# A decoder trunk on one core: down products in two halves of 256 columns, their stationary tiles shifted by 128 bytes, and one wide step per block

## The chip, the core and the metric

The kernel runs on one core of a Trainium2 chip. TensorE (PE in the profile) multiplies, VectorE (DVE) and ScalarE (ACT) work on what it makes, GpSimd (POOL) and SyncE (SP) mostly issue transfers. The metric is the device time of one execution in microseconds, the median of several. Before the change it is 1897.52 us (three runs, 1895.87 to 1897.72).

## The reference

Two layers over 512 tokens of 1024 features in float32. Each layer is: half-step SwiGLU feed-forward, token mixer (differential attention in layer 0, pooling in layer 1), cross-attention into 256 memory tokens, and a second half-step SwiGLU; after each, a layer norm of `a * x + ...`. So there are four feed-forward blocks, and the change touches these alone:

```python
def swiglu_ffn(x, w_in, w_out):
    h = x @ w_in                       # 1024 -> 2 x 2816
    g, u = jnp.split(h, 2, axis=-1)
    return (jax.nn.silu(g) * u) @ w_out   # 2816 -> 1024
```

## The kernel before

**Products in three passes.** Every float32 operand is split into a high part (a cast on ACT) and a low part (a subtraction on DVE). A product is then three matmuls, high by high, high by low, low by high, all into the same PSUM bank:

```python
def mm3(self, out, w, x, start, stop, again=False):        # L227
    self.first_mm = mm(out, w[0], x[0], ...)                # L231
    mm(out, w[0], x[1], ...)                                # L232
    self.last_mm = mm(out, w[1], x[0], ...)                 # L233
```

`w` is the stationary operand (a slice of 128 columns, 512 bytes per partition, which PE loads ahead of the matmul) and `x` the moving one. In the profile's rows an instruction stands as `out<-moving,stationary`.

**A feed-forward block.** The hidden width is cut into 11 units of 256. Products are not done plainly: seven products of sub-blocks take the place of eight, on the up side (`up`, seven products x, y, z of 24 matmuls each with 256 moving columns) and on the down side (`down`, for two units at a time, seven steps px, py, pz). In an up product the weights wh, wl are stationary and the factors of x (xh, xl, or the tiles xe) move. In a down step it is the reverse: h (tiles ha and hb) is stationary and the weights move, 512 columns at a time. A down step is two products (b = 0, 1) of two contraction chunks (k = 0, 1) of three passes, so 12 matmuls; DVE adds each product's bank to the tokens X (L935).

**The order of work.** `FFN_TURNS` gives five turns: three units up; then four turns with two units up and, beside them, the down steps of two earlier units. Units 8, 9 and 10 go down at the end of the block in plain products (`plain_down`, ps). The generators of a turn are stepped one after the other (the loop of `ffn` from L629), which puts on PE: 24 matmuls of one unit, 24 of the other, one down step, and again. A turn has seven such rounds; in the last turn the last two down steps stand among plain products. So a block has 4 turns x 7 = 28 down steps, the kernel 112, with 1344 matmuls. A scheduler behind the program then places every instruction on its engine's queue; `queue_behind(a, b)` makes `a` stand behind `b` on one engine.

**Places in memory.** Tiles lie one behind the other. `APART["ffn"]` is 64, `ROUND` 512: a pad of 64 bytes ahead of the weights (`to_w`), and one of 448 ahead of x's factors (`_x`, `to_x`). With them the weights start at 32 modulo 512 bytes, all factors of x at 480, and the tiles behind xe (hb, sp, ha, sr, hr) at 480 too. All tiles and slices used here are multiples of 512 bytes long, so a tile's start tells where each of its slices lies modulo 512.

Of the kernel before, what the change touches and what calls it, by code (L numbers as in the profile page):

```python
# [17 lines left out]
P = 128  # L18
D = 1024
S = 512  # L20
# [26 lines left out]
    turn=(1.0, 1.0, 1.2, 1.5),  # L47
# [79 lines left out]
class Trunk:  # L127
# [49 lines left out]
    @contextmanager  # L177
    def phase_pool(self, gain, spare, **bufs):

        self.gain, self.spare, self.bufs, self.phase = gain, spare, bufs, {}
        with ExitStack() as ctx:
            for t in bufs:
                if t == "_x":
                    self.to_x(ctx)
                elif t == "_w":
                    self.to_w(ctx)
                else:
                    self.phase[t] = self.stage.get(t) or ctx.enter_context(self.pool(t))  # L190
            yield
# [378 lines left out]
    def ffn(self, layer, j, ln, beside=()):  # L570
        w_in, w_out = self.a["ffn_w_in"][layer, j], self.a["ffn_w_out"][layer, j]
        self.seven_of, self.factors = {}, self.factor_tiles()
        nc, n, beside = self.nc, len(FFN_TURNS), iter(beside)
        at_start = bool(self.load_rest)
        downs = {i: self.down(d, w_out, 2.0 * ALPHA if i == 1 else 1.0) for i, (_, d) in enumerate(FFN_TURNS) if d}

        def start(turn):
            ups = FFN_TURNS[turn][0]

            early = (2, 1, 1) if turn == 0 else (0, 0)  # L580
            rest = self.load_rest.pop if turn == 0 and at_start else lambda: lambda: None
            got = [self.up(w_in, u, lane, early[lane], rest() if lane == 0 else None) for lane, u in enumerate(ups)]
            for lane, g in enumerate(got):
                next(g)
                if lane == 1:
                    rest()()
            if turn > 1:
                next(downs[turn])
            return got + [downs[i] for i in downs if i == turn]

        works = start(0)
        if at_start:

            zeros = self.act("hb", (P, P + S), mybir.dt.bfloat16)
            nc.vector.memset(zeros, 0.0)
            idle = self.aux("idle", "yz")
            self.warm(zeros, idle, 7)
            for tag, half in (("px", 0), ("py", 1)):
                for t in self.late[:2]:
                    self.turn(t, half, tag)  # L600
                if half == 0:
                    with self.tc.issue_after(self.last_turn.ins):
                        self.warm(zeros, idle, 9)
                next(works[0])
                if half == 0:
                    next(works[0])
            next(works[1])
        else:
            for w in works + works[:1]:
                next(w)  # L610
            self.turn_late(2)
        self.late = []
        next(works[0])
        act, dve = self.first_split
        if self.begins:

            for late, first in zip(self.begins, (act, dve)):
                self.queue_behind(late, first)
        second = self.second_factors()
        if at_start:  # L620

            next(works[0])
            for w in (works[1], second, second, works[1], works[2], works[2], works[0]):
                with self.behind():
                    next(w)
        else:
            for w in (second, *works[1:], second, downs[1]):
                next(w)
        for turn in range(n):  # L629
            behind = turn == n - 1  # L630
            for step in range(1 if turn == 0 else 0, 9 if behind else 7):
                if turn == 0 and (step == 3 or step == 2 and at_start):
                    next(second)
                if step == 4:
                    if behind:
                        coming = [self.plain_down(w_out, layer, j, ln, beside)]
                    else:
                        coming = start(turn + 1)
                        if at_start and turn == 0:
                            with self.tc.issue_after(self.last_load.ins):  # L640
                                next(downs[1])
                if behind and step in (4, 6, 7, 8):
                    next(coming[0])
                if behind and step > 3:
                    few(beside, 2)

                for lane, w in enumerate(works[: None if not behind or step > 1 else -1]):
                    if not (at_start and turn == 0 and lane < 2 and step == 1):
                        next(w, None)
                    if turn == 0 and lane == 1 and step == 2 and at_start:  # L650
                        next(works[0])
                    if turn == 0 and lane == 0 and step == 2 and not at_start:
                        next(second)
                    if at_start and turn == 0 and lane == 0 and step == 3:
                        next(works[2])
                if turn == 1 and step == 3:
                    self.seven_of[self.waiting[0]] = self.seven(self.waiting[1])
            works = coming
        drain(works[0])
# [63 lines left out]
    def up(self, w, u, lane, early, between):  # L723
# [28 lines left out]
        def product(ps, v, a, start=False, passes=False):  # L752
            if passes or between and start and a == 0:
                by_passes(ps, v, a)
                return
            x = self.factors[a]
            for j in range(2):
                o = slice(j * P, (j + 1) * P)
                for k in range(4):

                    self.mm3(
                        ps[:, j], (v[0][:, k, o], v[1][:, k, o]), (x[0][:, k], x[1][:, k]),
                        start and j == k == 0, j == 1 and k == 3, True,
                    )

        def by_passes(ps, v, a, which=range(3)):

# [14 lines left out]
        at_start = early > 0 and self.begins is None  # L782
        sp = lambda: self.tmp("ha" if third else "sp", (P, 2, H))
# [38 lines left out]
        hr = self.tmp("hr", (P, 2, S))  # L822
# [73 lines left out]
    def down(self, pairs, w, scale):  # L896
# [24 lines left out]
        def product(ps, b, a, ws, start=False):  # L921

            o = slice(b * P, (b + 1) * P)
            for k in range(2):
                h, l = hs[k][a]
                self.mm3(ps, (h[:, o], l[:, o]), ws[k], start and k == 0, k == 1, not start)

        started = set()

# [802 lines left out]
        return self.stage_pools(5, dict(raw=raw), order)  # L1732

    def ffn_phase(self, **more):
        bufs = dict(b1=1, b3=1, b2=1, b4=1, _x=0, xe=6, hb=4, sp=4, ha=4, sr=1, hr=3)
        return self.phase_pool(("hr", "sr"), "sp", **bufs, **more)

    def ffn_first(self, layer, ln):
# [84 lines left out]
```

## Time and profile before

| | before |
|---|---|
| median of the runs | 1897.52 us |
| the profiled execution | 1899.25 us |
| its span, first to last instruction | 1897.5 us |
| granted TensorE clock | 0.999 |
| PE busy | 1886.5 us in 13120 matmuls |
| DVE busy | 1540.9 us (81%) |
| ACT busy | 1000.8 us (53%) |
| POOL busy | 308.2 us (16%) |
| HBM | 147 GB/s over the span |

PE's busy time is the union of its matmuls' modelled spans, which overlap: a busy PE need not be at its best pace. What a matmul costs in a full stream is the distance between the starts of neighbours, read from the rows in order of time.

### The profile page before, as it was taken

The page shows a single profiled execution, that of the slowest core. Times are in us where ns is not written, and L with a number is a line of the kernel's source. Part 1 is how long each engine was busy: PE and PEld are TensorE (multiplying, and loading weights), DVE is VectorE, ACT ScalarE, POOL GpSimd, SP SyncE. Part 2 cuts the span into 40 slices and gives each one's busy share as a digit, 9 for nine tenths or more (in the row PEclk, how much of TensorE's full clock was granted, in tenths as well). Part 3 has the DMA queues.
Part 4 walks back from the last instruction along what each step waited for, and adds up shares of the span by engine and source line. Part 5 has one row for each costly group of instructions (what it writes and reads, how often), then busy time and mean ns, then how long its engine had stood idle before and what let it go on. Part 6 is the DMA issues. An engine that isn't in the chain of part 4 may idle for free.

```text
span 1897.5 us, 32589 instructions
## 1 busy us (share of the span) xinstructions
PE 1886.5 (99%) x13120; PEld 1730.9 (91%) x13120; DVE 1540.9 (81%) x2246; ACT 1000.8 (53%) x1542; POOL 308.2 (16%) x274
## 2 busy tenths in 40 slices
PE   9999999999999999999999999999999999999998
PEld 8999998888889988999998999999899889999996
DVE  7888989888876558889887988898786568998886
ACT  6555554566654435555554655555455436555552
POOL 3112120112110002221220311212120012211210
PEclk9999999999999999999999999999999999999999
DMA  9978772322235327987785687777464438867861
GB/s 254 215 178 178 171 141 85 103 69 75 91 112 178 112 70 181 195 177 168 144 188 168 118 179 181 168 166 162 157 172 146 142 69 180 173 159 178 185 129 53
DMA packets 250055, 283.20 MB, mean 149 GB/s; under 512 B 8752, under 2 KB 213040, under 8 KB 249904
## 3 DMA queue, kind: packets, MB, share of 16 engines
q0 software_dynamic: 94080, 94.38, 32.3%
q1 hardware_dynamic: 155824, 186.74, 30.2%
q8 instruction: 103, 1.69, 0.4%
q14 instruction: 48, 0.39, 0.1%
HBM read 274.79 MB, written 4.19 MB: 147 GB/s over the span
## 4 chain that ended last, share of the span: by engine, by line
PE 96%; DMA 2%; DVE 1%; ACT 0%; SPq 0%; issue 0%; POOL 0%; DVEq 0%; ACTq 0%
PE x L231 7%; PE x L232 7%; PE x L233 7%; PE ps L231 5%; PE ps L233 4%; PE ps L232 4%; PE z L231 4%; PE z L233 4%; PE z L232 4%; PE px L233 3%; PE px L231 3%; PE px L232 3%; PE x L773 3%; PE y L231 2%; PE y L232 2%; PE y L233 2%
## 5 line engine op out<-in xcount | busy, mean ns | idle before, releaser
L741 POOL DMA_DIRECT2D ra<-in_ffn_w_in_dram x132 | 170.7, 1307 | 977.6 <-DVE wl L748 960.4
L746 ACT CAST wh<-ra 128x1024 fp32r<-128x1024 f32 x176 | 184.9, 1053 | 197.8 <-PE x L232 63.8
L748 DVE TENSOR_TENSOR wl<-ra,wh 128x1024 fp32r<-128x1024 f32 x176 | 214.2, 1220 | 64.7 <-ACT wh L746 64.0
L231 PE MATMUL x<-xe,wh 128*128 128x256 f32 x704 | 195.0, 277 | 0.0
L232 PE MATMUL x<-xe,wh 128*128 128x256 f32 x704 | 194.8, 277 | 0.0
L233 PE MATMUL x<-xe,wl 128*128 128x256 f32 x704 | 194.8, 277 | 0.0
L746 ACT CAST wh<-rc 128x1024 fp32r<-128x1024 f32 x132 | 138.9, 1053 | 100.3 <-PE x L232 41.6
L143 ACT CAST wh<-b 128x1024 fp32r<-128x1024 f32 x112 | 117.8, 1052 | 134.8 <-PE x L232 62.2
L748 DVE TENSOR_TENSOR wl<-rc,wh 128x1024 fp32r<-128x1024 f32 x132 | 159.5, 1218 | 24.7 <-ACT wh L746 24.7
L144 DVE TENSOR_TENSOR wl<-b,wh 128x1024 fp32r<-128x1024 f32 x112 | 136.7, 1220 | 40.9 <-ACT wh L143 40.9
L231 PE MATMUL x<-xh,wh 128*128 128x256 f32 x536 | 148.7, 277 | 0.0
L232 PE MATMUL x<-xl,wh 128*128 128x256 f32 x536 | 148.4, 277 | 0.0
L233 PE MATMUL x<-xh,wl 128*128 128x256 f32 x536 | 148.4, 277 | 0.0
L231 PEld LDWEIGHTS x<-xe,wh 128*128 128x128 f32 x704 | 132.4, 188 | 1.3
L232 PEld LDWEIGHTS x<-xe,wh 128*128 128x128 f32 x704 | 132.3, 188 | 1.3
L233 PEld LDWEIGHTS x<-xe,wl 128*128 128x128 f32 x704 | 132.2, 188 | 0.0
L144 DVE TENSOR_TENSOR wl<-raw,wh 128x1024 fp32r<-128x1024 f32 x64 | 78.5, 1233 | 45.8 <-ACT wh L143 45.2
L231 PEld LDWEIGHTS x<-xh,wh 128*128 128x128 f32 x536 | 100.8, 188 | 0.7
L232 PEld LDWEIGHTS x<-xl,wh 128*128 128x128 f32 x536 | 100.8, 188 | 0.7
L233 PEld LDWEIGHTS x<-xh,wl 128*128 128x128 f32 x536 | 100.7, 188 | 0.0
L143 ACT CAST wh<-raw 128x1024 fp32r<-128x1024 f32 x64 | 66.4, 1049 | 62.5 <-PE xq L232 18.2
L231 PE MATMUL z<-xe,wh 128*128 128x256 f32 x352 | 97.5, 277 | 0.0
(445 smaller groups left out, 6239.9 us busy)
## 6 DMA issues: line engine op xcount, KB each, us to landing
ra<-in_ffn_w_in_dram POOLq DMA_DIRECT2D x132, 512.0 KB, 7.0
rc<-in_ffn_w_in_dram SPq DMA_DIRECT2D x88, 512.0 KB, 5.8
b<-in_ffn_w_out_dram SPq DMA_DIRECT2D x76, 512.0 KB, 5.0
ra<-in_ffn_w_in_dram SPq DMA_DIRECT2D x44, 512.0 KB, 4.7
rc<-in_ffn_w_in_dram POOLq DMA_DIRECT2D x44, 512.0 KB, 7.3
raw<-in_xa_wkv_dram SPq DMA_DIRECT2D x16, 1024.0 KB, 5.4
raw<-in_da_w_qkv_dram SPq DMA_DIRECT2D x24, 512.0 KB, 3.7
raw<-in_xa_wq_dram SPq DMA_DIRECT2D x8, 1024.0 KB, 5.2
```

The source lines that it names most:

```text
L143: self.nc.scalar.copy(hi, src),
L144: self.nc.vector.tensor_sub(lo, src, hi.bitcast(F32)),
L231: self.first_mm = mm(out, w[0], x[0], start=start, stop=False, skip_group_check=again)
L232: mm(out, w[0], x[1], start=False, stop=False, skip_group_check=again)
L233: self.last_mm = mm(out, w[1], x[0], start=False, stop=stop, skip_group_check=again)
L741: nc.gpsimd.dma_start(t, source(*block), accum_op=ALU.add)
L746: hi = nc.scalar.copy(v[0], raw)
L748: lo = nc.vector.tensor_sub(v[1], raw, v[0].bitcast(F32))
L773: self.last_mm = nc.tensor.matmul(ps[:, j], v[i][:, k, j * P : (j + 1) * P], x[l][:, k], start=n == i == l == 0, stop=n == 7 and i == 1, s ...
```

## The change

Three edits in the feed-forward blocks. The sums are the same in another grouping.

- A down product that was 512 columns wide is done in two halves of 256, with the same two contraction chunks in each: 24 matmuls for a step in place of 12.
- A new pad of 128 bytes stands behind the tiles xe (`_h`). It moves hb, sp, ha, sr and hr from 480 to 96 modulo 512, so that h's slices lie 64 bytes above the weights in place of 64 below.
- The first step of a block's first down (turn 1; in the first block, `at_start`, also that of turn 2) stays 512 columns wide. Its very first matmul has to stand ahead of the last five three-pass products of the up product before it, that is 15 matmuls earlier. To this end `up` keeps the first matmuls of its last product in `up_mms`.

```diff
@@ phase_pool
+                elif t == "_h":
+                    self.pad(ctx, 2 * self.apart)
@@ ffn, in the loop over steps
+                self.ahead = step == 0 and 0 < turn < 2 + at_start
                 for lane, w in enumerate(works[: None if not behind or step > 1 else -1]):
@@ up, product
             x = self.factors[a]
+            self.up_mms = []
...
+                    self.up_mms.append(self.first_mm)
@@ down, product
             o = slice(b * P, (b + 1) * P)
-            for k in range(2):
-                h, l = hs[k][a]
-                self.mm3(ps, (h[:, o], l[:, o]), ws[k], start and k == 0, k == 1, not start)
+            cols = (0, S) if self.ahead else (0, 2 * P, S)
+            for c, e in zip(cols, cols[1:]):
+                for k in range(2):
+                    h, l = hs[k][a]
+                    self.mm3(
+                        ps[:, c:e], (h[:, o], l[:, o]), [w[:, c:e] for w in ws[k]],
+                        start and c == k == 0, k == 1 and e == S, True,
+                    )
+                    if self.ahead and b == k == 0:
+                        self.queue_behind(self.up_mms[-5], self.first_mm)
@@ ffn_phase
-        bufs = dict(b1=1, b3=1, b2=1, b4=1, _x=0, xe=6, hb=4, sp=4, ha=4, sr=1, hr=3)
+        bufs = dict(b1=1, b3=1, b2=1, b4=1, _x=0, xe=6, _h=0, hb=4, sp=4, ha=4, sr=1, hr=3)
```

What stands on PE where the first block's first down step begins, before (the last up product x of the first turn, then the step px):

```order
L232 MATMUL x<-xl,wh 128x256
L233 MATMUL x<-xh,wl 128x256
L231 MATMUL px<-wh,ha 128x512
L232 MATMUL px<-wl,ha 128x512
L233 MATMUL px<-wh,ha 128x512
```

and at the same place now (mm3's three lines are L233 to L235 there):

```order
L234 MATMUL x<-xl,wh 128x256
L235 MATMUL x<-xh,wl 128x256
L233 MATMUL px<-wh,ha 128x512
L233 MATMUL x<-xh,wh 128x256
...
L235 MATMUL x<-xh,wl 128x256
L234 MATMUL px<-wl,ha 128x512
L235 MATMUL px<-wh,ha 128x512
```

One 512-column matmul moved into the up product, and five products of three passes (15 matmuls, the rows left out among them) now follow it before the other eleven of the step.

The step after that one on PE (py, between the up products y and z), before:

```order
L233 MATMUL y<-xh,wl 128x256
L231 MATMUL py<-wh,ha 128x512
L232 MATMUL py<-wl,ha 128x512
L233 MATMUL py<-wh,ha 128x512
...
L231 MATMUL z<-xh,wh 128x256
```

and now:

```order
L235 MATMUL y<-xh,wl 128x256
L233 MATMUL py<-wh,ha 128x256
L234 MATMUL py<-wl,ha 128x256
L235 MATMUL py<-wh,ha 128x256
...
L233 MATMUL z<-xh,wh 128x256
```

Its place is the same; between its neighbours stand 24 matmuls of 256 columns where 12 of 512 stood. The 107 narrow steps all look like this. On SP and POOL the order is as it was; on DVE and ACT some splits and additions of neighbouring units change places.

## The prediction

> **What bounds the kernel now.** I read the page first, then the waits, then the chain of waits, and last the matmuls in order of time.
>
> ```profile
> span 1897.5 us, 32589 instructions
> PE 1886.5 (99%) x13120; PEld 1730.9 (91%) x13120; DVE 1540.9 (81%) x2246; ACT 1000.8 (53%) x1542; POOL 308.2 (16%) x274
> PE 96%; DMA 2%; DVE 1%; ACT 0%; SPq 0%; issue 0%; POOL 0%; DVEq 0%; ACTq 0%
> ```
>
> The third row is the chain that ended last: 96% of it is PE. PE's own waits are few; these are the two longest, in microseconds in total, times, longest.
>
> ```profile
> PE idle L138 <- DVE hb L595: 1.3, 1, 1.3
> PE ps L231 <- DVE X L380: 0.8, 1, 0.8
> ```
>
> So the end moves by what the stream of matmuls takes. A row's own length does not say that, because matmuls overlap; the distance from one start to the next does. Hence the timeline of PE (start in us, modelled length, engine, line, out<-moving,stationary), first and last rows of stretches whose matmuls I counted:
>
> ```profile
> 85.09 0.39 PE L231 MATMUL py<-wh,ha 128*128 128x512 f32 x1
> ...
> 117.94 0.39 PE L231 MATMUL px<-wh,hb 128*128 128x512 f32 x1
> ...
> 120.69 0.28 PE L231 MATMUL x<-xh,wh 128*128 128x256 f32 x1
> ...
> 121.28 0.28 PE L233 MATMUL x<-xh,wl 128*128 128x256 f32 x1
> ...
> 126.16 0.39 PE L231 MATMUL px<-wh,hb 128*128 128x512 f32 x1
> ...
> 241.14 0.39 PE L231 MATMUL px<-wh,hb 128*128 128x512 f32 x1
> ```
>
> From 85.09 to 241.14 lie 19 rounds, each one down step (12 products of 512 columns) and two up products (48 of 256): 156.05/19 = 8.213 us a round. Inside one: 117.94 to 120.69, 12 matmuls, 2.75 us, 229.0 ns each. Then 5 matmuls to 121.28 at 118 ns, then 43 to 126.16 at 113.3 ns. So after every 512-column step the 256-column stream runs slowly for five matmuls, 5 x 5 = 0.026 us, and then settles.
>
> Two paces of the same 256-column up product:
>
> ```profile
> 45.73 0.28 PE L231 MATMUL x<-xe,wh 128*128 128x256 f32 x1
> ...
> 76.71 0.28 PE L233 MATMUL x<-xh,wl 128*128 128x256 f32 x1
> ...
> 747.01 0.28 PE L232 MATMUL y<-xl,wh 128*128 128x256 f32 x1
> ...
> 796.88 0.28 PE L231 MATMUL x<-xh,wh 128*128 128x256 f32 x1
> ```
>
> 45.73 to 76.71 is 263 matmuls, 117.8 ns each; 747.01 to 796.88 is 440, 113.3 ns each. Nothing in these stretches waits, operands and addresses modulo 512 are alike (moving 480, stationary 32). The stream has a long and a short pace and stays in the one it is in; the first down step, which follows 76.71, ends the long one, since the rounds from 85.09 on settle at the short one. The round of 8.213 us is 2.75 + 48 x 113.3 ns + 0.026.
>
> **The change part by part.** *Down steps in pairs.* 1284 of the 1344 down matmuls become 2568 of 256 columns. In the short pace 24 of them take 24 x 113.33 = 2.720 us against 2.748 now (8.213 less 5.440 and 0.026), and the five slow matmuls behind the step go, because no width changes any more: 72 x 113.33 = 8.160 us a round, 0.053 less. Whether they run at 113.3 rests on addresses: in the up product the stationary slice lies 64 bytes above the moving one (32 against 480 modulo 512), in the down step it lies 64 below (480 against 32), and the pad of 128 bytes puts it 64 above (96 against 32). So pairs with that pad look to PE like more up products. Of 112 steps 107 are narrow; 99 are followed by up products, 8 (the last two of each block) by plain products. 99 x 0.053 = 5.25, 8 x 0.028 = 0.22, together -5.5 us.
>
> The Trainium skill says the opposite of the halving: "Larger matmuls are more efficient than smaller matmuls, when possible" (Perfetto Trace Analysis, Matmuls), and TensorE: Matmul & The Clock Gate, Back-to-back issue gap, gives N/2.4 + 2.5 ns. By that two halves cost 218.3 ns against 215.8, and 1284 halvings add 3.3 us. The rows differ from it, 229.0 against 2 x 113.3 = 226.7, and they decide.
>
> *The pad.* It moves all tiles of hb, sp, ha, sr and hr by 128 bytes; of these only h feeds PE. The wide steps stay at 512 columns with the slice 64 above. The rows nearest to that are another stage's 512-column products, whose weights lie 64 above x:
>
> ```profile
> 1456.08 0.39 PE L231 MATMUL xq<-xh,wh 128*128 128x512 f32 x1
> ...
> 1458.41 0.39 PE L232 MATMUL xq<-xl,wh 128*128 128x512 f32 x1
> ```
>
> Ten matmuls, 2.33 us, 233 ns: 4 ns more than now, 60 x 4 = 0.25 us; the other bound is no change. The plain products of the blocks' second half have hb and ha moving and xe stationary; these were level and will be 128 apart.
>
> ```profile
> 312.65 0.39 PE L231 MATMUL ps<-ha,xe 128*128 128x512 f32 x1
> ...
> 314.01 0.39 PE L231 MATMUL ps<-hb,xe 128*128 128x512 f32 x1
> ```
>
> Level they take 1.36/6 = 227 ns. There are 270 such products of 512 columns. No row has 128 apart; bounds are 227 and 233, 0 to +1.7 us. The row at hand for these very products is the lower end, so I take a third, +0.6.
>
> The Trainium skill holds that PE has two independent read ports, and loading the next weights takes nothing from the running matmul (TensorE: Matmul & The Clock Gate, Step-by-step: what each phase is for). By it the pad would be worth nothing and the sum would keep only the halving. 113.3 and 117.8 ns for one product say that something is shared, though not what.
>
> *The first product ahead.* In five steps one 512-column matmul goes 15 matmuls (1.7 us) forward. It needs the cast of the weights and of h, not their low halves, and nothing in these rows waits at that place. ACT is 53% busy. It makes one more change of width, so one more slow group of five: 5 x 0.026 = 0.13 us. Bounds: 0, if the group is absent, and 0.26 if it comes on both sides.
>
> *Queues.* Transfers keep their order on SP and POOL, so none of them is late by it; some DVE instructions change places. DVE has room in most turns, but not in the last turn of the first block.
>
> ```profile
> 277.00:285.00 8.00, 8.00 (x61) 7.55 (x60) 8.00 (x11) 3.39 (x4) 0.00 (x0) 1.00 0.21 44
> 285.00:293.00 8.00, 8.00 (x61) 7.51 (x60) 8.00 (x13) 3.65 (x4) 0.00 (x0) 1.00 0.06 24
> ...
> 297.90 0.39 PE L231 MATMUL ps<-wh,xe 128*128 128x512 f32 x1
> 298.39 0.47 PE L231 MATMUL px<-wh,hb 128*128 128x512 f32 x1
> ```
>
> The columns of the first two are length, PE, PEld, DVE, ACT, POOL, clock, DMA share, GB/s: DVE is busy all 8.00 us, and PE stands still at 298 (0.49 us between starts, 0.23 is usual). What PE gains there, five rounds, 0.27 us, it waits for at 298 instead. I give back 0.3. In the other turns no wait of PE was listed, so nothing is given back there.
>
> *Sum.* -5.5 + 0.25 + 0.6 + 0.13 + 0.3 = -4.2 us. The profiled execution took 1899.25 us (span 1897.5 and 1.75 around it), 1.7 above the median of the runs, 1897.52; against the median the forecast is **1893.3 us**.
>
> **The rivals.** *Slow groups stay.* If the boundaries between up and down upset the pace as a change of width does now, each costs 0.026 us: one a round leaves 99 x 0.027 + 0.2 = 2.9 of the 5.5, so 1895.9 with the same +1.3; two a round leave 0.2, so 1898.6. For it: moving and stationary addresses jump at both boundaries. Against: within up products, where tiles change too but not the offset, no such group appears from 747 to 797.
>
> *The long pace is caught and kept.* This ends on the other side. One boundary of this kind is in the trace: the moving weights change to being the stationary ones, as from a down step to an up product.
>
> ```profile
> 1425.88 0.28 PE L233 MATMUL pk<-mem4h,wl 128*128 128x256 f32 x1
> ...
> 1427.24 0.28 PE L233 MATMUL ps<-wh,pooled 128*128 128x256 f32 x1
> 1427.36 0.28 PE L231 MATMUL pk<-mem4h,wh 128*128 128x256 f32 x1
> ...
> 1431.24 0.28 PE L231 MATMUL xq<-xh,wh 128*128 128x256 f32 x1
> ```
>
> Before it 12 matmuls at 113.5 ns, behind it 33 at 117.8 ns, all of 256 columns, and behind it the stationary slice lies 64 above. If every down step does this to the up products behind it, a round costs 24 x 113.3 + 48 x 117.8 ns = 8.374, 0.161 more than now: 99 x 0.161 + 1.1 = +17, 1914.6. If only the down steps run long, 2.827 + 5.440 + 0.026 = 8.293: +0.080 x 99, 1906.5, or 1904 without the slow group. If both do, 72 x 117.8 = 8.482: +0.269 x 99, about 1925. It decides from the first boundary that is not undone: the gain of 0.053 a round is lost when 12 matmuls in 72 run long. Against: behind 512-column steps, at the same boundary, all rounds from 85 to 241 settle; the one example had its slice 64 below ahead of the boundary, the changed kernel has it above on both sides.
>
> *DVE takes it.* PE may merely wait more (81% busy, nearly 100% in the first block's last turn); what all rounds gain would come back as waits: 1897 to 1898.
>
> **How the numbers follow.** About 0.2%, 3.8 us, is what a measurement of this kernel can tell from no change. The forecast case gets 0.60, its own range 1891.5 to 1896 from the bounds above; its middle lies just beyond 3.8, so I count 0.46 of it as faster and 0.14 as the same. Slow groups 0.11 and DVE 0.04 are the same. The long pace gets 0.25, split 0.09 (down only), 0.09 (up only), 0.07 (both). Faster 0.46, same 0.29, slower 0.25. The forecast case, the small rivals and the down-only case hold 0.84; that reaches to 1905, and 1890.5 below leaves the pad's unknown price a little room.
>
> **What would show it.** Rounds of 8.16 us between the starts of narrow steps; 113.3 ns for 24 down matmuls in a row; no five matmuls at 118 behind them; about 233 ns in the wide steps. A round of 8.21 speaks for slow groups, above 8.25 for the long pace, and which of the two products runs at 117.8 says which boundary. More PE waits on DVE with rounds of 8.16 inside would mean that the gain was real and spent elsewhere. If the plain products pass 233 ns, my price for the pad was too low.

## The result

The changed kernel takes 1912.0 us (median, 1910.7 to 1914.9), the kernel before beside it 1897.6: a ratio of 1.0078, 95% interval 1.0065 to 1.0091. The change makes the kernel 0.8% slower; the forecast was 1893.3.

The page of the changed kernel, its span, its engines and its chain of waits:

```profile
span 1910.3 us, 35144 instructions
PE 1896.1 (99%) x14404; PEld 1791.5 (94%) x14404; DVE 1542.6 (81%) x2246; ACT 1000.1 (52%) x1542; POOL 307.9 (16%) x274
PE 92%; DVE 3%; DMA 2%; ACT 1%; issue 1%; SPq 0%; POOL 0%; DVEq 0%; ACTq 0%; POOLq 0%
```

DVE, ACT and POOL work as long as before. The span grew by 12.8 us, and PE is still what bounds it. Its timeline (start, modelled length, engine, line, out<-moving,stationary) at the place of the first quoted round, and at both ends of twelve later rounds:

```profile
85.24 0.28 PE L233 MATMUL py<-wh,ha 128*128 128x256 f32 x1
...
88.06 0.29 PE L233 MATMUL z<-xh,wh 128*128 128x256 f32 x1
...
88.42 0.28 PE L233 MATMUL z<-xh,wh 128*128 128x256 f32 x1
...
93.52 0.28 PE L233 MATMUL pz<-wh,hb 128*128 128x256 f32 x1
...
143.24 0.28 PE L233 MATMUL py<-wh,ha 128*128 128x256 f32 x1
...
242.68 0.28 PE L233 MATMUL px<-wh,hb 128*128 128x256 f32 x1
```

From 143.24 to 242.68 lie twelve rounds of 8.287 us, where the kernel before had 8.213. Inside one, the 24 narrow down products take 2.82 us (85.24 to 88.06), 117.5 ns each: the long pace, not the short one of 113.3. Behind them three up products are slow (0.36 us to 88.42, 120 ns each), and the other 45 need 113.3 (88.42 to 93.52). It is the same in all four blocks.

The second place is at the end of the first block, where PE waits 2.4 us. That wait and one of 0.6, at 1371.95 in the third block, stand out against the waits of the kernel before. Here are these two of PE's waits, and then the rows of PE around the longer one:

```profile
PE px L233 <- DVE X L947: 2.4, 1, 2.4
...
PE ps L234 <- DVE hb L144: 0.6, 1, 0.6
```

```profile
299.89 0.40 PE L233 MATMUL ps<-wh,xe 128*128 128x512 f32 x1
302.71 0.36 PE L233 MATMUL px<-wh,hb 128*128 128x256 f32 x1 [2.43 <-DVE X L947]
...
316.98 0.40 PE L233 MATMUL ps<-ha,xe 128*128 128x512 f32 x1
...
318.37 0.40 PE L233 MATMUL ps<-hb,xe 128*128 128x512 f32 x1
```

The last two rows are the start of six plain products of ha and xe and the row behind them: 1.39 us, 232 ns each, 227 before.

I added up the distances from start to start over all matmuls of both traces, by the kind of product. Down products: 308.1 us before (1344 of 512), 316.1 now (2568 of 256 and 60 of 512), +8.0. Plain products with weights moving, which hold both waits above (a wait counts with the row ahead of it): +3.6. Plain products with h moving: +0.9. All else together: +0.3. That is the 12.8 us of the profiled execution; the medians lie 14.4 apart.

### The profile page after: what moved, and what is told of

It reads as the page before. It is cut to its first block, busy times and chain, and to the rows that moved or that the text cites. A ratio compares the mean times of both kernels' runs of the same rounds, so it can differ in the third digit from the quotient of the medians.

```text
span 1910.3 us, 35144 instructions
## 1 busy us (share of the span) xinstructions
PE 1896.1 (99%) x14404; PEld 1791.5 (94%) x14404; DVE 1542.6 (81%) x2246; ACT 1000.1 (52%) x1542; POOL 307.9 (16%) x274
## 4 chain that ended last, share of the span: by engine, by line
PE 92%; DVE 3%; DMA 2%; ACT 1%; issue 1%; SPq 0%; POOL 0%; DVEq 0%; ACTq 0%; POOLq 0%
PE x L233 7%; PE x L235 7%; PE x L234 7%; PE z L233 4%; PE z L235 4%; PE z L234 4%; PE ps L233 4%; PE ps L234 4%; PE ps L235 4%; PE px L233 3%; PE px L235 3%; PE px L234 3%; PE x L778 3%; PE y L233 2%; PE y L235 2%; PE y L234 2%
## 5 line engine op out<-in xcount | busy, mean ns | idle before, releaser
L233 PE MATMUL x<-xe,wh 128*128 128x256 f32 x704 | 194.9, 277 | 0.0
L235 PE MATMUL x<-xe,wl 128*128 128x256 f32 x704 | 194.7, 277 | 0.0
L143 ACT CAST wh<-b 128x1024 fp32r<-128x1024 f32 x112 | 117.7, 1051 | 131.2 <-PE x L234 63.7
L233 PE MATMUL x<-xh,wh 128*128 128x256 f32 x536 | 148.7, 277 | 0.0
L235 PE MATMUL x<-xh,wl 128*128 128x256 f32 x536 | 148.4, 277 | 0.0
L235 PEld LDWEIGHTS x<-xe,wl 128*128 128x128 f32 x704 | 132.4, 188 | 0.0
L233 PEld LDWEIGHTS x<-xe,wh 128*128 128x128 f32 x704 | 132.1, 188 | 0.0
L233 PE MATMUL px<-wh,hb 128*128 128x256 f32 x384 | 108.0, 281 | 2.7 <-DVE X L947 2.4
L235 PE MATMUL px<-wh,hb 128*128 128x256 f32 x384 | 107.8, 281 | 0.0
L234 PE MATMUL px<-wl,hb 128*128 128x256 f32 x384 | 107.8, 281 | 0.0
L235 PEld LDWEIGHTS x<-xh,wl 128*128 128x128 f32 x536 | 100.7, 188 | 0.0
```

Of the source, the lines that this page charges most:

```text
L143: self.nc.scalar.copy(hi, src),
L233: self.first_mm = mm(out, w[0], x[0], start=start, stop=False, skip_group_check=again)
L234: mm(out, w[0], x[1], start=False, stop=False, skip_group_check=again)
L235: self.last_mm = mm(out, w[1], x[0], start=False, stop=stop, skip_group_check=again)
```

## Experiments

The pads and widths below are edits of the changed kernel. "Offset" is how far the stationary slice lies above the moving data, modulo 512; in the change it is +64 in up products and +64 in down steps, before it was +64 and -64.

**One part at a time.** Four kernels: without the pad, with the pad alone, without the wide step, and with only the second product of each step (b = 1) in halves.

```diff
e1  -  ... xe=6, _h=0, hb=4 ...          +  ... xe=6, hb=4 ...
e2  -  cols = (0, S) if self.ahead else (0, 2 * P, S)     +  cols = (0, S)
e2, e3, e4  -  self.ahead = step == 0 and 0 < turn < 2 + at_start     +  self.ahead = False
e4  -  cols = (0, S) if self.ahead else (0, 2 * P, S)     +  cols = (0, S) if b == 0 else (0, 2 * P, S)
```

> The change without the pad of 128 bytes: in the down step h's slice lies 64 below the weights (480 against 32) as before the change, the halves and the wide step stay. The changed kernel has rounds of 8.29 us: 24 down products at 117.7 ns, 48 up products at 113.3 with three slow ones. Theory E (entry: the long pace is caught where the up product gives way to the down step, where the new slice lies 128 above the data that moves; here it would be level with it): the down products keep the short pace, 113.3 ns, rounds 8.16 to 8.19, time 1895 to 1898 with the 2.4 us wait on DVE that the change brought. Theory P (places within the step: moving weights at 32 with the slice at 96 make a long pair): with the slice below it may be either, 113.3 or 117.7. Theory N (no place matters: what is long is a 256-column product whose moving operand is a weight tile, or whose bank is written in two halves): 117.7 ns, rounds 8.29, time about 1911, which is 1912.0 less the 1.0 us that the plain products of h and xe lost by the pad.

> The pad alone: all down steps 512 columns wide as before, nothing ahead, h at 96. In the changed kernel the 60 wide products took 232.4 ns each against 229.3 before. If that is the pad's price for every wide product, 1344 x 3.1 ns = 4.2 us, and the plain products of h and xe lose 1.0 more: 1902.8, rounds 8.25. If the 232.4 came from the switches of width around the few wide steps, rounds stay 8.21 and the time is 1898.6. DVE's order is the one of before, so no 2.4 us wait in the first block's last turn under either.

> The change with all 112 steps narrow and nothing ahead. Theories E, P and N agree on the down steps: 117.7 ns, rounds 8.29. Five wide steps of 2.79 us become narrow ones of 2.83 (+0.2), and the slow groups around them go (-0.1 to -0.2): 1912.0, within 1. If the wide step and its product ahead are what brought DVE's 2.4 us wait in the first block's last turn, 1909.5.

> Pad kept, nothing ahead; of each down step the first product (b = 0, six matmuls) is 512 columns wide and the second (b = 1) is two halves, twelve matmuls of 256. So the narrow products are entered from wide ones, as the up products of before are, which settle at 113.3 after five. Theory E: of the twelve, five at 118 and the rest at 113.3, no slow group in the up products behind: step 2.78 us, round 8.22. Theory P and theory N: all twelve at 117.7, step 2.81, three slow up products behind, round 8.27; time 1905 to 1907, under theory E 1901 to 1903 (1897.6, +2.1 for the wide halves, +1 for plain products, 0 to +2.4 for the wait).

| run | ratio to before | 95% interval |
|---|---|---|
| e1, pairs without pad | 1.0089 | 1.0074 to 1.0104 |
| e2, pad alone | 1.0085 | 1.0068 to 1.0102 |
| e3, all steps narrow, pad | 1.0055 | 1.0040 to 1.0070 |
| e4, second product narrow, pad | 1.0048 | 1.0033 to 1.0063 |

e1 falls outside all three theories. Its PE rows, the starts of a down step and of the up products behind it, two rounds in a row:

```profile
85.40 0.28 PE L233 MATMUL py<-wh,ha 128*128 128x256 f32 x1
...
88.12 0.28 PE L233 MATMUL z<-xh,wh 128*128 128x256 f32 x1
...
93.78 0.28 PE L233 MATMUL pz<-wh,hb 128*128 128x256 f32 x1
...
96.61 0.28 PE L233 MATMUL z<-xe,wh 128*128 128x256 f32 x1
...
102.06 0.28 PE L233 MATMUL pz<-wh,hb 128*128 128x256 f32 x1
```

The first step takes 2.72 us (113.3 ns a product) and the up products behind it 5.66 (117.9); the next step takes 2.83 (117.9) and its up products 5.45 (113.5). So it goes on, round by round, to the block's end: the products, places and widths are the same, and the pace alternates. An offset or a product does not have a pace; the stream is in a state, and the boundary from up to down keeps it here while the boundary from down to up turns it.

e2's time, 1915.4, lies beyond both of its expectations, and it shows the same thing where nothing is halved. Again the starts of down step and up products:

```profile
85.98 0.39 PE L233 MATMUL py<-wh,ha 128*128 128x512 f32 x1
...
88.77 0.28 PE L233 MATMUL z<-xh,wh 128*128 128x256 f32 x1
...
94.42 0.39 PE L233 MATMUL pz<-wh,hb 128*128 128x512 f32 x1
...
97.22 0.28 PE L233 MATMUL z<-xe,wh 128*128 128x256 f32 x1
...
102.69 0.39 PE L233 MATMUL pz<-wh,hb 128*128 128x512 f32 x1
```

The up products take 5.65 us behind the first step and 5.47 behind the second, in turn. The pad costs about 16 us by itself: 11.7 us in up products, none of which it moves, 5.1 in the wide steps (233 ns a product instead of 229) and 1.0 in the plain products of h.

e4 holds both pictures in one kernel. Its narrow half, the up products behind it, and the next step, in the first block and in the second:

```profile
86.38 0.28 PE L233 MATMUL py<-wh,ha 128*128 128x256 f32 x1
...
87.74 0.28 PE L233 MATMUL z<-xh,wh 128*128 128x256 f32 x1
...
93.40 0.40 PE L233 MATMUL pz<-wh,hb 128*128 128x512 f32 x1
...
814.82 0.28 PE L233 MATMUL py<-wh,ha 128*128 128x256 f32 x1
...
816.23 0.29 PE L233 MATMUL z<-xh,wh 128*128 128x256 f32 x1
...
821.70 0.39 PE L233 MATMUL pz<-wh,hb 128*128 128x512 f32 x1
```

In the first block twelve narrow products take 1.36 us (short) and 48 up products 5.66 (long); in the second 1.41 (long) and 5.47 (short). All 25 rounds of the first block run the one way, all of the others the other way. The first block came in from its long stretch of up products, the others from short ones. So neither theory E nor P nor N holds for it, though its time, 1907.9, is near that of P and N.

e3 has the rounds of 8.287, and its time, 1909.4, is the one expected if the wide step brought the whole wait on DVE. But the wait only falls from 2.4 to 1.6:

```profile
PE px L233 <- DVE X L947: 1.6, 1, 1.6
```

Of the 2.9 us by which e3's span is shorter than the change's, 1.3 lie in the plain products and their waits and 1.2 in up products, above all in the first block's stretch ahead of its first down step, which runs at 113.3 ns here and at 117.8 in the change. So the number was hit in part by luck.

**Other offsets.** The pad was set to 64, 192, 256 and 96, all steps narrow, one execution each.

```diff
-                    self.pad(ctx, 2 * self.apart)
+                    self.pad(ctx, 64)      # e6: 192, e7: 256, e11: 96
```

> All steps narrow, nothing ahead, and a pad of 64 in place of 128: in the down step h's slice is level with the weights (32 against 32), and the first slice of a step lies 64 above the up data before it. Theory E is changed by the first four runs into theory F (two phases): PE's stream of 256-column products is in one of two phases, each boundary either keeps or turns it, and which of them is short depends on the places. Pad 128: both boundaries turn (up short, down long, up short). No pad: up to down keeps, down to up turns (113 and 118 alternate from step to step). F, for an offset not seen yet, allows three patterns: nothing turns in sum and both streams short, 8.16 us a round, about 1897 (1909.4 less 99 x 0.127); nothing turns in sum and one stream long, 8.29 (1909.4) or 8.37; one turn a round, alternating, mean 8.33, about 1914. Theory P, the offset within each stream alone decides: one pace for all down steps and one for all up products, the same in every round of every block, never an alternation.

> As the run with the pad of 64, with 192: the slice 128 above the weights in the down step, the entry 192 above the up data. Theory F: one of the three patterns (8.16, 8.29 or 8.37, or alternating with a mean of 8.33); if the phase goes by even and odd multiples of 64, the same pattern as with the pad of 64. Theory P: one pace per stream throughout.

> As the two before, with 256: the slice 192 above the weights, the entry 256 above the up data. Theory F: one of the three patterns; if the entry's distance modulo 256 decides, the pattern of no pad, an alternation with a mean round of 8.33, about 1914 with all steps narrow. Theory P: one pace per stream throughout.

> All steps narrow, nothing ahead, weights and x as in the change, pad of 96: h at 64, the slice 32 above the weights. Theory F with the two phases living only at odd multiples of 64: neither pattern; like the pads of 64 and 192 (even multiples) a fixed down pace of 118 to 120 and up products that settle at 113.3 in every round, 8.30 to 8.32, about 1910 to 1914. If the grain is coarser than 64, the pattern of the pad of 128 (8.287, 1909.4) or of no pad with an alternation.

Measured: 1914.8, 1910.9, 1916.0 and 1910.6 us. With 64, 192 and 96 (offsets 0, 128 and 32) every round is alike, 8.32, 8.30 and 8.29 us; the down products take 119.2, 118.4 and 118.2 ns on the mean, and the up products always settle at 113.3. With 256 (offset 192, which is -64 modulo 256) short and long alternate as without pad. So e7 and e11 came out as theory F had them; e5 and e6 have the steady paces that theory P asks for. In these runs and those above, the down step is seen at both paces with offsets -64, +64 and 192, which are odd multiples of 64; at the others tried, 32 among them, it has one pace, a slow one, also in the one block that came in long (the third of e5). Larger pads were not tried.

**The mirror.** Weights' and x's pads exchanged, so that the up products have offset -64; h so that the down step has 192 (e9) or +64 (e10). All steps narrow, one execution each.

```diff
-APART, ROUND, LINE = {"ffn": 64, "da": 448, "pool": 64}, 512, 480
+APART, ROUND, LINE = {"ffn": 448, "da": 448, "pool": 64}, 512, 480
e9   -  self.pad(ctx, 2 * self.apart)         +  self.pad(ctx, 128)
e10  -  ... xe=6, _h=0, hb=4 ...              +  ... xe=6, hb=4 ...
```

> All steps narrow, nothing ahead, and the pads ahead of weights and x exchanged: weights at 416 modulo 512, x at 480 (the slice 64 below the moving data in the up products), pad of 128 ahead of h (96: in the down step the slice 192 above, which modulo 256 is 64 below). Both streams have the slice below, where the change has it above in both. Theory F in the form that only the pair of offsets modulo 256 counts, mirrored or not: the picture of the change, one stream at 113.3 and the other at 117.7 in every round, 8.29 us, about 1909 to 1911 (or 8.44 if the up products are the long ones, 1925). Theory B (the boundary turns or keeps by itself, and here it may keep twice): both short, 8.16, about 1897.

> As the run before without the pad ahead of h (h at 480: the slice 64 above the weights in the down step, 64 below the moving data in the up products). It is the mirror of the run of pairs without pad. Theory F, mirrored: short and long alternate from round to round, mean 8.33 us, about 1914. Theory B: another pattern, 8.16 (1897) if both boundaries keep, 8.29 if both turn.

e10 took 1921.8 us where theory F had 1914: it alternates with the mean that was expected, a round of 8.17 (both short), then one of 8.49 (both long), but the up products ahead of the first down step run at 117.8 ns in all four blocks, and in the kernel before in the first block alone. Here the boundary from down to up keeps the pace and the other one turns it. e9 took 1937.8, with a picture that neither theory had: both streams long, always.

```profile
85.95 0.28 PE L233 MATMUL py<-wh,ha 128*128 128x256 f32 x1
...
88.77 0.28 PE L233 MATMUL z<-xh,wh 128*128 128x256 f32 x1
...
94.43 0.28 PE L233 MATMUL pz<-wh,hb 128*128 128x256 f32 x1
```

The step takes 2.82 us and the up products 5.66, 8.48 a round.

**Is it a state there too?** If e9 only carried a long pace in from its beginning, one disturbance per block should make it short for good. All four are edits of e9. e13 made the first step of each block wide; e14 also put its first product ahead; e15 left out one of two dropped 512-column matmuls at the start of the later blocks; e16 kept a single wide product, ahead, and the rest of that step narrow.

```diff
e13, e14, e16  self.ahead = step == 0 and turn == 1
e13  -  if self.ahead and b == k == 0: self.queue_behind(...)
e15  -  for _ in range(2):                        +  for _ in range(1):
e16  +  first = nc.tensor.matmul(ps, hs[0][a][0][:, o], ws[0][0], start=start, stop=False, ...)
     +  self.queue_behind(self.up_mms[-5], first)
     (the other two products of that pass, and all behind them, in halves)
```

> The kernel of both slices below (weights at 416, x at 480, h at 96), in which down and up ran long in every round (8.48 us), with one edit: the very first down step of each block is 512 columns wide, nothing ahead. Theory F (the pace is a state that lives on; in this layout both boundaries keep it): a single wide step per block, which turns the state as wide steps did in the run of the pad alone, makes all narrow rounds behind it short, 8.16 to 8.18 us, in place of 8.48: about 1937.8 - 99 x 0.31 = 1907. Rival R (in this layout the long pace belongs to the places, not to a state): 8.48 in all narrow rounds, 1937.6.

> As the run before, and the first product of the wide step 15 ahead, as in the change. The single wide product and the eleven others are two switches of width where the run before has one. Theory F: if each switch turns, the two undo each other and rounds stay at 8.48 (1937.8); if a group of wide products sets the pace rather than turns it, rounds are the same as in the run before. Rival R: 8.48.

> The kernel of both slices below, all steps narrow; ahead of each later block's product y stand two 512-column matmuls whose result is dropped (weights moving, a slice of the same weights stationary, level): one of them is left out. Theory F, if a wide product turns the state: the three later blocks run short from there on, up and down, rounds of 8.16 to 8.18, and the first block stays long; about 1937.8 - 3 x (25 x 0.31 + 2.2) = 1908. If level wide products set the state, or rival R: 8.48 everywhere and 1937.6 (0.24 us less per block).

> The kernel of both slices below (weights at 416, x at 480, h at 96), all products narrow but one: in each block the first product of the first down step is one matmul of 512 columns, 15 ahead, and the rest of that step is narrow. In the run with the whole wide step ahead, this single product brought the up products of the first block from 118 to 113 and those of the later blocks from 113 to 118, and the eleven wide ones behind it left all long. Theory F (a state that lives on; both boundaries keep it in this layout): in the first block, if its stretch ahead is long again, up and down run short behind the single product, 8.16 to 8.18 us a round for all 24 rounds, where the same places ran 8.48; in the later blocks, all short where the stretch ahead was long, all long where it was short. Rival R (these places always run long in down steps): down at 117.7 in every round of every block, rounds of 8.48, or 8.27 if only the up products go short.

They took 1938.2, 1935.3, 1936.3 and 1937.6 us, with narrow rounds of 8.48 in all. e16's rows around its single wide product tell why:

```profile
74.29 0.28 PE L233 MATMUL x<-xh,wh 128*128 128x256 f32 x1
...
75.35 0.39 PE L931 MATMUL px<-wh,ha 128*128 128x512 f32 x1
75.58 0.28 PE L233 MATMUL x<-xh,wh 128*128 128x256 f32 x1
...
77.17 0.28 PE L235 MATMUL x<-xh,wl 128*128 128x256 f32 x1
77.29 0.28 PE L941 MATMUL px<-wl,ha 128*128 128x256 f32 x1
...
79.88 0.28 PE L233 MATMUL y<-xh,wh 128*128 128x256 f32 x1
```

Ahead of it nine up products take 1.06 us, 118 ns each; behind it fourteen take 1.59 (75.58 to 77.17), 113.6: the same products of the same layout went from long to short. Then the down step comes, and its 22 products take 2.59 us, 117.7 each, and everything behind stays long. In the later blocks the up products came in long and stayed long behind the single product, which is not what theory F had. So the up products have a state here as well, but in this layout a down step is long whichever way it is entered, and the up products behind it too. Theory F had the state right and the boundary wrong.

**A reset, and what DVE makes of it.** In the kernel before, up products always settle behind a wide step with offset -64. e8 (no pad) keeps the second product wide and halves the first. e17 narrows all but the last three products of a step and leaves the first block as it was. e18 is e8 with one instruction of DVE in its old place.

```diff
e8   +  cols = (0, S) if b else (0, 2 * P, S)
e17  +  if not self.halves: cuts = [(k, 0, S) for k in range(2)]        # first block
     +  elif b == 0: cuts = [(k, c, c + 2 * P) for c in (0, 2 * P) for k in range(2)]
     +  else: cuts = [(0, 0, 2 * P), (0, 2 * P, S), (1, 0, S)]
e18  -  V.tensor_copy(ang, pi32)          +  self.pos_cast = V.tensor_copy(ang, pi32)
     +  self.queue_behind(self.pos_cast, lo)        # in up, behind the next split
```

> No pad, nothing ahead; of each down step the first product (b = 0) is two halves and the second (b = 1) stays 512 columns wide. In the kernel before, whose wide steps also have the slice 64 below, the up products behind always settle at 113.3 after five slow ones, even after the long stretch of the first block. Theory F with a reset: the entry keeps the short pace, twelve down products at 113.4 (1.361 us), six at 229 (1.374), 48 up products in 5.466: 8.20 us a round, 0.013 less than before, 112 x 0.013 = -1.4 us, 1897.3 with before at 1898.7, if no wait comes with it; up to 2 more with the waits on DVE that the halves bring in the first block's last turn. If the wide products don't reset but only turn the phase, rounds alternate between 8.20 and about 8.45.

> No pad, nothing ahead; the first block as before the change, 512 columns wide; in the three later blocks all of a down step is narrow but its last three products (b = 1, k = 1), which stay 512 wide. Theory F with a reset: eighteen products at 113.4 and three at 229 make a step of 2.728 us, the up products behind settle at 113.3 after five slow ones (5.466): rounds of 8.194 in the later blocks, 0.019 less than before, 84 steps x 0.019 = -1.6 us, and no wait on DVE in the first block, since its order is the one of before: ratio 0.9991. If three wide products don't set the short pace, short and long alternate as in the run of pairs without pad: about 8.31 on the mean, +8 us, ratio 1.004.

> The kernel with the first product of each step narrow and the second wide (e8: rounds of 8.200 us, ratio 0.9998), with one edit on DVE: in the last turn of the first block the cast of the positions (L1083) stands behind the split wl<-rc that followed it. In all kernels with halves that cast stands ahead of this split and DVE idles 1.0 to 1.9 us there until the transfer of the positions lands; before, the split stands ahead and DVE does not wait. Theory C (that idle time is the whole of PE's later wait on X<-X,px): PE's wait of 1.2 us goes to below 0.4, ratio 0.9992 (0.9998 less 1.2/1898). Rival: DVE is full there for other reasons (the halves change other places of its order too), and PE's wait stays at 1 us or more, ratio 0.9998.

e8's rows, step, up products, next step:

```profile
85.27 0.28 PE L233 MATMUL py<-wh,ha 128*128 128x256 f32 x1
...
88.01 0.28 PE L233 MATMUL z<-xh,wh 128*128 128x256 f32 x1
...
93.47 0.28 PE L233 MATMUL pz<-wh,hb 128*128 128x256 f32 x1
```

2.74 and 5.46 us: 8.20, as worked out, in all rounds of all blocks. All of e8's blocks came in short. In e18, which has the same steps, the first block came in long: its twelve narrow products run at 118 ns, and the up products behind the six wide ones settle at 113.3 all the same. So the wide products reset the pace and do not turn it. e8's time is that of before, 0.9998 (0.9989 to 1.0008). The 1.4 us gained in the rounds go to PE's waits, above all `px` on DVE, 1.2 us. e17's rounds are 8.193, three wide products are enough for the reset, and the wait in the first block is gone; but the ratio is 1.0021 (1.0012 to 1.0029). Its PE waits:

```profile
PE ps L234 <- DVE wl L144: 1.8, 2, 1.3
PE pp L1442 <- DVE pooled L144: 1.6, 2, 0.9
PE pk L235 <- DVE wl L144: 1.1, 1, 1.1
```

These 4.5 us stand in the token mixer behind the third block, where the kernel before waits for nothing of the kind; why DVE is late there was not tested.

e18 settles what the wait in the first block is. DVE's rows around the cast of the positions, of before, of the change and of e18:

```profile
273.13 1.22 DVE L748 TENSOR_TENSOR wl<-rc,wh 128x1024 fp32r<-128x1024 f32 x1
...
275.41 0.42 DVE L1071 CAST hr<-hr 128x512 f32<-128x512 int32 x1
```

```profile
274.76 1.22 DVE L924 TENSOR_TENSOR b<-b,b 128x1024 f32<-128x1024 f32 x1
277.86 0.43 DVE L1083 CAST hr<-hr 128x512 f32<-128x512 int32 x1 [1.87 <-DMA hr<-in_positions_dram]
278.20 1.22 DVE L751 TENSOR_TENSOR wl<-rc,wh 128x1024 fp32r<-128x1024 f32 x1
```

```profile
274.31 1.22 DVE L752 TENSOR_TENSOR wl<-rc,wh 128x1024 fp32r<-128x1024 f32 x1
275.44 0.42 DVE L1087 CAST hr<-hr 128x512 f32<-128x512 int32 x1
```

Before, the cast finds its transfer landed (4.3 us after its issue), and a split stands ahead of it. In the change it stands ahead of that split, the transfer lands 5.3 us after its issue, and DVE idles 1.87 us. With the one instruction put back (e18), PE's wait of 1.2 us on `px` is not in the list any more. Its ratio is 0.9995 (0.9986 to 1.0004): the best of all kernels here, and no difference that can be measured.

**The product ahead alone** (no pad, all steps 512 wide):

```diff
-  ... xe=6, _h=0, hb=4 ...                               +  ... xe=6, hb=4 ...
-  cols = (0, S) if self.ahead else (0, 2 * P, S)         +  cols = (0, S)
```

> The kernel before with only the third edit: all steps 512 columns wide, no pad, and in five steps the first product 15 ahead. The changed kernel was 1.0078 times before and the one without wide step 1.0055, so the wide step may cost up to 4 us. Theory W (it costs by waits: DVE's order is moved by it, and the last turn of the first block has no room): a wait of PE on DVE of more than 0.5 us near 298, ratio 1.0005 to 1.002. Theory S (a slow group more in five steps and nothing else): ratio 1.0000 to 1.0003, no new wait.

1.0010 (1.0001 to 1.0019), with rounds of 8.213 and two new waits: one in the step after the first wide one, at 84.91, and one at 299.13, where theory W had it.

```profile
PE py L234 <- DVE wl L144: 1.3, 1, 1.3
...
PE px L233 <- DVE X L947: 1.0, 1, 1.0
```

So it costs by waits (theory W): 2.3 us in these two, where the ratio says 1.9. The span of the profiled execution shows only 0.2 of it, because its up products take 2.2 us less than those of before, above all ahead of the first down step, where they run at 113.3 ns in place of 117.8. That stretch is short in e3, e5, e6, e8, e11, e12, e15 and e17 and long in all others; with one trace of each kernel, what decides it stays open, and differences of a tenth of a per cent between kernels could come from it.

The second wait comes from the cast of the positions too, though in e12 it stands behind its split as before:

```profile
276.14 0.43 DVE L1083 CAST hr<-hr 128x512 f32<-128x512 int32 x1 [0.84 <-DMA hr<-in_positions_dram]
```

Here the transfer lands 5.4 us after its issue. So the order is one reason for DVE's idle time, and a slower transfer is another.

## Why the prediction was wrong

**The failed step** is "pairs with that pad look to PE like more up products", and with it the term of -5.5 us. The narrow down products run at 117.5 ns, not 113.33: 2.82 us a step where 2.720 was forecast and 2.748 stood before. In e1, e4 and e10 the same product runs at either pace in one kernel. The prediction said itself that the stream "stays in the one it is in", and then priced the down step by its addresses alone, as if a like offset carried the short pace across the boundary. With +64 on both sides, as in the change and e3, every group of up products settles to short and every narrow step behind it runs long: the boundary turns the pace each time, and e4's first block shows the way back turning from short to long as well. No narrow step of these two kernels came behind long up products, so a boundary that always leads to long would look the same.

Two slips are small beside it. 100 of the 112 steps are followed by up products and 12 by plain ones, so 95 and 12 of the narrow steps (99 and 8 were taken), which makes the term -5.4. And 1284 halvings at 218.3 less 215.8 ns are 3.2 us, not 3.3.

**The five slow up products** were to go. Three of about 120 ns stay, so the 48 up products take 5.46 us against 5.47 before and 5.44 forecast: this part of the gain was nothing. It did not hang on a change of width.

**The rival that came true** is "the long pace is caught and kept", down steps alone: 8.27 to 8.29 us a round were worked out and 8.287 measured. It was given 0.09, and with its other terms 1904 to 1906.5, in place of 1912; 3.0 us of the rest are the two waits of PE. The one row that showed such a boundary, at 1427.36 before, has offset -64 ahead of it and +64 behind it, and turns a short pace into a long one. That is what e1 does from down to up at the same offsets. The row was a right witness, but for the kernel without pad; "against" it the prediction set the settling behind 512-column steps, and e8 and e17 show that settling to be the work of the wide products, which the change takes away.

**The pad**: 232.4 ns in the wide steps (233 taken) and +0.9 us in the plain products of h (+0.6 taken, 0 to 1.7 as bounds) are about the forecast. What it does to a pace was not in the price: alone it costs 0.85%, most of it in up products that it does not touch. The Trainium skill says of PE's reads that loading the next weights takes nothing from the running matmul, since each has a port of its own (TensorE: Matmul & The Clock Gate, Step-by-step: what each phase is for); the prediction said that the pad would be worth nothing by it. The measurement decides against that step, with 1.0085 for the 128 bytes of e2; whether it is the load that takes something from the running matmul, no run here shows.

**DVE in the first block's last turn**: 0.3 us were given back, and 2.4 were lost in one wait (the other, of 0.6, is in the third block). The reason offered, PE arriving early where DVE is full, was wrong, since PE arrives late. DVE loses time ahead of the turn that fills it. Three windows (length, PE, PEld, DVE, ACT, POOL, clock, DMA share, GB/s): the change around its cast, the kernel before at the same place of the program, which it reaches 1.7 us earlier, and the change from its cast to PE's wait.

```profile
269.00:285.00 16.00, 16.00 (x141) 16.00 (x140) 12.64 (x16) 8.11 (x9) 1.28 (x1) 1.00 0.51 91
```

```profile
267.30:283.30 16.00, 16.00 (x119) 15.02 (x118) 14.51 (x19) 8.23 (x9) 1.28 (x1) 1.00 0.49 84
```

```profile
278.00:302.00 24.00, 22.28 (x184) 21.51 (x182) 23.97 (x34) 11.46 (x13) 0.00 (x0) 1.00 0.20 67
```

DVE is busy 12.64 of 16 us, 14.51 before, and the difference is the 1.87 us of idle time ahead of the cast. From there on it is busy 23.97 of 24 us and cannot make up for it. The other traces agree: where the cast does not wait (before, e2, e17, e18), PE waits 0.1 us at most at this place; in the other sixteen the cast waits 0.8 to 2.0 us, and PE 0.2 (e4) to 2.4. The statement that transfers keep their order was true and did not help: what moved was the instruction that waits for one, and the transfer itself took longer. Moving that cast alone removed the wait in e18; in the change itself it was not tried, and by the rows above DVE would still idle 0.7 us there, an estimate (1.87 less the 1.13 us that the split holds DVE in the rows of e18).

**The product ahead** was priced at 0.13 us by its slow group and costs 0.2 to 3.6 by e12's interval.

**What bounds the kernel** was read rightly: the stream of PE, in which one pace of 4.5 ns decides.

## What to carry to other kernels

Two paces of the same instruction in one trace point to a state, and a state has no price per instruction: what counts is what each boundary of the new stream does to it, and a boundary can be priced only by a row with the same offsets on both sides, in the same direction, at the pace that comes in. Before a stream is cut finer, look for what now resets it, since the wide products that look slow (229 against 226.7 ns) may be what keeps the rest short. And where a scheduler orders an engine, follow not only the transfers but each instruction that waits for one.

## What was not expected of the hardware

The pace of 256-column float32 products is a state of the stream of weight loads and matmuls, and what a boundary does to it goes by the offsets on both sides:

| offsets, up / down | up to down | down to up | round |
|---|---|---|---|
| +64 / +64 (change, e3; e4 from down to up) | turns (seen from short alone) | turns | 8.287 |
| +64 / -64 or 192 (e1, e7) | keeps | turns | 8.28 and 8.38 |
| -64 / +64 (e10) | turns | keeps | 8.17 and 8.49 |
| -64 / 192 (e9, e16) | to long | long stays | 8.48 |
| +64 / 0, 32, 128 (e5, e11, e6) | one slow pace | to short | 8.29 to 8.32 |

Only h was moved, or the weights' and x's pads exchanged, so no run separates these differences from the places themselves.

Wide products act on the state too. At the end of a step with offset -64, three, six or twelve of them set the up products behind them short (e17, e8, before), also from a long pace (e18, before). With +64, twelve of them turn it (e2), but the change's eleven, entered short, leave it short. A single one, ahead of its step, leaves the fifteen up products behind it short with +64 (the change: 117.8 before it in the first block, 113.3 in the others) and long with -64 (e1 and e12, behind 113.3 and in e1's first block behind 117.8). With 192 it leaves them short in the first block of e14 and e16, where they came in long, and long in all later blocks, where one group came in short and five long; what differs between the blocks there, no run shows.

No layout tried has both streams short in every round, which would be 8.16 us. What in PE or in its reads makes the 4.5 ns, none of these runs shows.
